# Half of a token tile's up side moved from matmuls to gathered rows

## The chip, the core and the metric

The kernel runs on one core of a Trainium2 chip. TensorE multiplies matrices (PE in the rows; PEld are its weight loads), VectorE (DVE) and ScalarE (ACT) work on elements, GpSimd (POOL) issues the gathers, SyncE (SP) issues most other transfers. The metric is the device time of one execution in microseconds; the kernel before takes 1613.15 us, the median of three runs (1612.51 to 1615.19).

## What is computed

One decoder layer on 512 tokens of width 1024, in float32: adaptive scale and shift, two kinds of attention, output projection, a norm, and then PEER, a layer of 16384 one-row experts. Each token has 8 heads, each head picks 16 experts, and the layer sums over these 128 picks:

```python
q = (hx @ w_pq).reshape(PEER_CHUNK, PEER_HEADS, 2, PEER_HALF)
sc = jnp.einsum('thpd,hpnd->thpn', q, sub_keys)
v_half, i_half = lax.top_k(sc, PEER_TOPK)
...
top_s, top_pos = lax.top_k(cand, PEER_TOPK)
idx = jnp.take_along_axis(cand_idx, top_pos, axis=-1)
g = jax.nn.softmax(top_s, axis=-1)
a = jax.nn.gelu(jnp.einsum('thkd,td->thk', u_tab[idx], hx))
return jnp.einsum('thk,thkd->td', (g * a), v_tab[idx])
```

`u_tab` is the up side (one dot product for a token and an expert), `v_tab` the down side (one row added for a token and an expert). A second norm ends the layer.

## The kernel before

The 512 tokens are four tiles of 128 (t = 0 to 3). Attention, the output projection and the first norm run first; `post_x` writes each tile's normed rows and, for tile 0, the expert layer's input `h2` by rows to memory. The product-key stage then multiplies by `w_pq`, and VectorE finds the best 16 of each half (`top16`). The first up blocks already stand beside it.

The expert stage treats tile 0 and tiles 1 to 3 in two ways.

Tiles 1 to 3 go densely over all 16384 experts, in 128 blocks of 128. An up block (`u_block`) loads 512 KB of `u_T`, splits it into a high and a low float32r part (`split`: ScalarE L80, VectorE L81), does 24 matmuls of 384 moving columns into the bank `st` (`mm3`, L90 to L92: three products for each of eight pieces of the width), and ScalarE's GELU writes the activations `a_r` (L756). A down block (`v_block`) loads and splits 512 KB of `v_blk`, multiplies the activations with the gate for each token and expert (`w`, L811), splits that too (L816, L817), and `v_mm` does 18 matmuls of 512 columns into six banks that add up over all blocks.

The dense gate comes from `topk` (the selection of one tile: indices `i01` and weights `g`) and `make_g`: for eight tokens at a time VectorE makes one-hot matrices (L671, L673), ScalarE scales one of them with eight instructions (L677), TensorE multiplies them, and ScalarE and VectorE copy the result to `stage` (L684), which goes to `g_d` in memory. Each such eight tokens is a gate unit; a tile has 16. `g_load` reads the gates back for eight blocks at a time.

Tile 0 takes its experts by gather (`gather_tile`): for each of the 128 picks, GpSimd's indirect transfer (L722) brings one row of `u_tab` to each of the 128 tokens, VectorE makes the dot product (L728), and later rows of `v_tab` are added with their weights (L738), in a ring of four buffers.

Three loops set the order. The first runs NB + NS = 32 + 24 up blocks ahead; after each, generators give out some of the selections, of the gate units (GRATE = 1.25 a block) and of the gathers, by a budget in microseconds (`pull`). Activations of 32 blocks stay in a ring; those of NS blocks go to `a_d` in memory by SP's queue (`keep`). The second part runs 72 pairs of an up and a down block with a gather budget of 3.2 us a pair, and the last 56 down blocks run alone with 1.2 us each. All engines take their instructions in a fixed order; `paced` ties the gathers' arithmetic to the blocks.

Of the kernel before, what the change touches and what calls it, by code (L numbers as in the profile page):

```python
# [20 lines left out]
P = 128  # L21
D = 1024
S = 512
# [15 lines left out]
NS = 24  # L39
GRATE = 1.25  # L40
LAST = 6


@with_exitstack
def layer(ctx: ExitStack, tc: tile.TileContext, A, out, dbg=None):
# [18 lines left out]
    h2_d = dram.tile([P, D], F32, name="h2_d")  # L64
    g2_d = dram.tile([1, D], F32, name="g2_d")
    a_d = [dram.tile([P, TD], F32, name=f"a_d{e}") for e in range(NS)]
# [431 lines left out]
    def post_x(t, pre, x1):  # L498
        nc.vector.tensor_mul(x1, pre, ln1g)
        nc.vector.tensor_add(x1, x1, ln1b)  # L500
        dma(x1_d[t], x1)
        if "x1" in dbg:
            dma(dbg["x1"][t * P:(t + 1) * P, :], x1)
        if t == 0:
            sc2row = row_of(lt, scale2, "rowtmp")
            h2 = pre
            nc.vector.tensor_mul(h2, x1, sc2row)
            sh2row = row_of(lt, cols(3), "rowtmp")
            nc.vector.tensor_add(h2, h2, sh2row)
            dma(h2_d, h2)  # L510
            g2row = row_of(lt, cols(5), "rowtmp")
            dma(g2_d, g2row[0:1, :])

    ln = {}
# [20 lines left out]
    sel = ctx.enter_context(tc.tile_pool(name="sel", bufs=1, reuse_waits="tile"))  # L535
# [50 lines left out]
    psB = ctx.enter_context(tc.tile_pool(name="psB", bufs=1, space=bass.MemoryType.PSUM, reuse_waits="tile"))  # L586
    ring_stack = ExitStack()
    ring = ring_stack.enter_context(tc.tile_pool(name="ring", bufs=1, side="right", reuse_waits="tile"))
    gath = ctx.enter_context(tc.tile_pool(name="gath", bufs=1, reuse_waits="tile"))
# [3 lines left out]
    def accbank():  # L593
        return psB.tile([P, 512], F32, name="acc", tag="acc", bufs=6)

    def topk(t, pool):
# [32 lines left out]
        i01 = sel.tile([P, 2, H, K16], F32, name="i01", tag="i01", bufs=2)  # L629
# [13 lines left out]
        g = sel.tile([P, H, K16], F32, name="g", tag="g", bufs=2)  # L643
# [49 lines left out]

    def all_topk(pool):
        for t in (1, 0, 2, 3):
            best[t] = yield from topk(t, pool)

    def all_g(pool, tk):
        for t in range(1, NT):
# [4 lines left out]
    acc0 = gath.tile([P, D], F32, name="acc0")  # L704
    h2n = gath.tile([P, D], F32, name="h2n")
    dma(h2n, h2_d)

    def gather_tile(pool):
        i01, g = best[0]
        ef = gath.tile([P, P], F32, name="ef")  # L710
        nc.vector.scalar_tensor_tensor(ef, i01[:, 0].rearrange("p h k -> p (h k)"), float(NKEY),
                                       i01[:, 1].rearrange("p h k -> p (h k)"), op0=OP.mult, op1=OP.add)
        ei = gath.tile([P, P], I32, name="ei")
        nc.vector.tensor_copy(ei, ef)
        w0 = gath.tile([P, P], F32, name="w0")
        nc.vector.tensor_copy(w0, g.rearrange("p h k -> p (h k)"))
        dots = gath.tile([P, P], F32, name="dots")
        yield 0.6

        def fetch(tab, j):  # L720
            b = gath.tile([P, D], F32, name="gb", tag="gb", bufs=4)
            nc.gpsimd.indirect_dma_start(out=b, out_offset=None, in_=A[tab],  # L722
                                         in_offset=bass.IndirectOffsetOnAxis(ap=ei[:, j:j + 1], axis=0))
            return b

        for j in range(P):
            b = fetch("u_tab", j)
            paced(nc.vector.scalar_tensor_tensor(b, b, 1.0, h2n, op0=OP.mult, op1=OP.mult,  # L728
                                                 accum_out=dots[:, j:j + 1]))
# [224 lines left out]
```

## Time and profile before

| what | value |
|---|---|
| median of three runs | 1613.15 us |
| the profiled execution, its span | 1615.1 us |
| TensorE, matmuls busy | 1536.0 us (95%) |
| VectorE busy | 1247.1 us (77%) |
| ScalarE busy | 760.0 us (47%) |
| GpSimd busy | 378.1 us (23%) |
| moved by DMA | 394.98 MB, mean 245 GB/s |

The shares are averages over stages with different work. Matmuls are pipelined and their ends are modelled, so the pace of TensorE is better read from their starts. A busy share of the DMA engines can come out a little over 1 in a short stretch.

### The profile page before, as it was taken

To read this page: it belongs to the slowest core of one execution; us is meant where nothing else is said; L and a number is where in the kernel's file an instruction comes from. 1 tells how busy PE (TensorE), PEld (TensorE's weight loads), DVE (VectorE), ACT (ScalarE), POOL (GpSimd) and SP (SyncE) were. 2 spreads that over 40 slices of the span, in tenths; PEclk is the share of its full clock that TensorE was granted. 3 is DMA by queue.
4 is the path that set the end of the run, shared out by engine and by line. 5 is a ranking of instruction groups with operands and counts; after the bars stand their busy time and mean duration, and the time that the engine had idled before them with its cause. 6 is when DMAs were issued, how large, how long until landed. Compare 5 with 4: busy or idle time off the path is not lost.

```text
span 1615.1 us, 22297 instructions
## 1 busy us (share of the span) xinstructions
PE 1536.0 (95%) x7837; PEld 1340.0 (83%) x7837; DVE 1247.1 (77%) x2519; ACT 760.0 (47%) x1346; POOL 378.1 (23%) x274
## 2 busy tenths in 40 slices
PE   7999898999998989998899999999999999999997
PEld 5677776889888888998788999988988898888875
DVE  7897666999898887766777777777868776787687
ACT  2565533234897998963233333333333333333341
POOL 0000000000011010104444443444535442434200
PEclk9999999999999999999999999999999999999999
DMA  8855542223366465689989889899889996889962
GB/s 302 289 187 181 170 156 82 89 79 116 107 219 213 155 232 190 219 282 359 313 304 329 291 311 319 297 321 312 320 289 324 322 306 246 286 300 310 374 204 76
DMA packets 154497, 394.98 MB, mean 245 GB/s; under 512 B 12305, under 2 KB 69009, under 8 KB 151186
## 3 DMA queue, kind: packets, MB, share of 16 engines
q1 hardware_dynamic: 117522, 259.33, 47.2%
q0 software_dynamic: 36864, 134.23, 23.0%
q8 instruction: 61, 1.00, 0.2%
q14 instruction: 50, 0.41, 0.1%
HBM read 358.91 MB, written 34.61 MB: 244 GB/s over the span
## 4 chain that ended last, share of the span: by engine, by line
PE 62%; issue 10%; DVE 10%; ACT 9%; DMA 7%; POOL 2%; SPq 0%; DVEq 0%; POOLq 0%; ACTq 0%
PE acc L91 9%; PE acc L90 9%; PE acc L92 9%; PE st L92 6%; PE st L91 6%; PE st L90 6%; ACT go L677 5%; PE bank L90 4%; PE bank L91 4%; PE bank L92 4%; DMA raw<-u_T 2%; DMA a_b<-a_d 2%; DVE lo L81 2%; ACT stage L684 1%; POOL gb L722 1%
## 5 line engine op out<-in xcount | busy, mean ns | idle before, releaser
L80 ACT CAST hi<-raw 128x1024 fp32r<-128x1024 f32 x286 | 300.3, 1051 | 359.8 <-PE st L91 191.3
L81 DVE TENSOR_TENSOR lo<-raw,hi 128x1024 fp32r<-128x1024 f32 x286 | 348.3, 1219 | 94.8 <-ACT hi L80 94.4
L90 PE MATMUL st<-h2h,hi 128*128 128x384 f32 x1024 | 352.4, 344 | 9.7 <-ACT a_r L756 5.8
L92 PE MATMUL st<-h2h,lo 128*128 128x384 f32 x1024 | 350.9, 343 | 5.6 <-DVE lo L81 5.5
L91 PE MATMUL st<-h2l,hi 128*128 128x384 f32 x1024 | 349.5, 341 | 0.0
L722 POOL DMA_INDIRECT gb<-u_tab,ei x128 | 173.2, 1353 | 623.2 <-DVE gb L728 354.6
L91 PE MATMUL acc<-lo,wh 128*128 128x512 f32 x768 | 304.3, 396 | 3.2 <-DVE lo L81 3.0
L90 PE MATMUL acc<-hi,wh 128*128 128x512 f32 x768 | 303.5, 395 | 0.4 <-ACT hi L803 0.4
L92 PE MATMUL acc<-hi,wl 128*128 128x512 f32 x768 | 303.8, 396 | 0.0
L722 POOL DMA_INDIRECT gb<-v_tab,ei x128 | 194.9, 1523 | 269.8 <-DVE acc L738 250.5
L90 PEld LDWEIGHTS st<-h2h,hi 128*128 128x128 f32 x1024 | 196.2, 192 | 15.2 <-ACT a_r L756 7.4
L816 ACT CAST wh<-w 128x384 fp32r<-128x384 f32 x128 | 65.6, 514 | 292.0 <-PE acc L91 273.6
L92 PEld LDWEIGHTS st<-h2h,lo 128*128 128x128 f32 x1024 | 196.0, 191 | 8.3 <-DVE lo L81 8.3
L91 PEld LDWEIGHTS st<-h2l,hi 128*128 128x128 f32 x1024 | 196.0, 191 | 3.2
L91 PEld LDWEIGHTS acc<-lo,wh 128*128 128x128 f32 x768 | 144.3, 188 | 36.5 <-DVE lo L81 4.3
L92 PEld LDWEIGHTS acc<-hi,wl 128*128 128x128 f32 x768 | 144.3, 188 | 34.5
L817 DVE TENSOR_TENSOR wl<-w,wh 128x384 fp32r<-128x384 f32 x128 | 71.1, 556 | 131.5 <-ACT wh L816 131.5
L90 PEld LDWEIGHTS acc<-hi,wh 128*128 128x128 f32 x768 | 144.1, 188 | 32.4 <-ACT hi L803 0.8
L677 ACT ACTIVATE go<-oh,iT 128x128 f32<-128x128 bf16 x384 | 166.4, 530 | 5.9 <-DVE eq L637 3.2
L738 DVE SCALAR_TENSOR_TENSOR acc<-gb,w,acc 128x1024 f32<-128x1024 f32 x127 | 162.2, 1277 | 1.2 <-DMA gb<-v_tab,ei 1.1
L728 DVE SCALAR_TENSOR_TENSOR gb<-gb,h2n 128x1024 f32<-128x1024 f32 x128 | 154.1, 1217 | 7.6 <-DMA gb<-u_tab,ei 7.5
L681 PE MATMUL acc<-go,oh 128*128 128x128 f32 x768 | 123.1, 294 | 15.2 <-ACT go L677 10.2
(206 smaller groups left out, 1854.5 us busy)
## 6 DMA issues: line engine op xcount, KB each, us to landing
raw<-u_T SPq DMA_DIRECT2D x128, 512.0 KB, 5.2
raw<-v_blk SPq DMA_DIRECT2D x128, 512.0 KB, 4.5
wada<-w_adaT SPq DMA_DIRECT2D x48, 512.0 KB, 4.5
g_d<-stage SPq DMA_DIRECT2D x24, 1024.0 KB, 5.4
gl<-g_d SPq DMA_DIRECT2D x16, 1536.0 KB, 13.1
raw<-w_pqT SPq DMA_DIRECT2D x16, 512.0 KB, 3.5
raw<-w_inT SPq DMA_DIRECT2D x10, 512.0 KB, 4.3
a_d<-a_r SPq DMA_DIRECT2D x24, 192.0 KB, 4.1
```

The costliest lines, as they stand in the source:

```text
L80: nc.scalar.copy(hi, src)
L81: split.last = nc.vector.tensor_sub(lo, src, hi.bitcast(F32))
L90: nc.tensor.matmul(ps, lh, rh, start=first, stop=False)
L91: nc.tensor.matmul(ps, lh, rl, start=False, stop=False)
L92: nc.tensor.matmul(ps, ll, rh, start=False, stop=last)
L677: nc.scalar.activation(go[:, i, :], oh0[:, :, i], AF.Copy, scale=iT[:, 2, t0 + i:t0 + i + 1])
L681: nc.tensor.matmul(ps[:, i * P:(i + 1) * P], oh1[:, 4 * u + i, :], go[:, 4 * u + i, :], start=True, stop=True)
L722: nc.gpsimd.indirect_dma_start(out=b, out_offset=None, in_=A[tab], in_offset=bass.IndirectOffsetOnAxis(ap=ei[:, j:j + 1], axis=0))
L728: paced(nc.vector.scalar_tensor_tensor(b, b, 1.0, h2n, op0=OP.mult, op1=OP.mult, accum_out=dots[:, j:j + 1]))
L738: paced(nc.vector.scalar_tensor_tensor(acc0, b, w0[:, j:j + 1], acc0, op0=OP.mult, op1=OP.add))
L816: nc.scalar.copy(wh, w)
L817: pace[0], pace_next[0] = pace_next[0], nc.vector.tensor_sub(wl, w, wh.bitcast(F32))
```

## The change

The first 64 tokens of tile 1 leave the up matmuls, which now take the last 320 tokens (`T0U` = 192 to 512). Their 128 picks are dot products with gathered rows instead: since 64 tokens fill half of the partitions, each gather brings two experts of a token at once (picks 0 to 63 to partitions 0 to 63, picks 64 to 127 to the others), so that 64 gathers do (`gather_part`). The GELU of the dots, multiplied into tile 1's gate weights, enters `make_g(1)`: the dense gate of these tokens is then already weighted, and `v_block` copies it (on ScalarE) where the other columns are multiplied. The down side is dense for them as before.

So that this can be, tile 1 is selected first and its gate is built last; the order of selections is 1, 2, 3, 0. 32 + 56 = 88 up blocks run ahead (before 56), the gate units are spread at 0.8 a block, and the activations of the 56 go out from a ring of three buffers of their own, by ScalarE's queue. Gate loads go by ScalarE's queue too, one group ahead. The gather ring has five buffers. Budgets: 2.2 us a block for the new gathers, then 1.3 us; 3.6 us a pair; 1.9 us for a down block alone. While blocks run ahead, the banks are four for `st` and four for the rest; then two and six as before.

```diff
-NS = 24
-GRATE = 1.25
+NS = 56
+GRATE = 0.8
+HU = 64
+T0U = P + HU
+TU = S - T0U
+GBUF = 5
+RA = 2.2
+RB = 1.3
...
-        for t in (1, 0, 2, 3):
+        for t in (1, 2, 3, 0):
             best[t] = yield from topk(t, pool)
+            if t < 2:
+                lists[t] = numbers(t)
...
+    def gather_part():
+        ei = lists[1]
+        eip = gath.tile([P, HU], I32, name="eip")
+        nc.vector.tensor_copy(eip[0:HU], ei[0:HU, 0:HU])
+        dma(eip[HU:P], ei[0:HU, HU:P])
+        for r in range(2):
+            dma(h2n[r * HU:(r + 1) * HU], h2_d[1][0:HU])
+        dots = gath.tile([P, HU], F32, name="dots1")
+        for j in range(HU):
+            dot(fetch("u_tab", eip, j), dots[:, j:j + 1])
+            yield 1.25
+        nc.scalar.activation(dots, dots, AF.Gelu)
+        far = gath.tile([P, HU], F32, name="far")
+        dma(far[0:HU], dots[HU:P])
+        g = best[1][1].rearrange("p h k -> p (h k)")
+        nc.vector.tensor_mul(g[0:HU, 0:HU], g[0:HU, 0:HU], dots[0:HU])
+        nc.vector.tensor_mul(g[0:HU, HU:P], g[0:HU, HU:P], far[0:HU])
+        weighted.append(True)
+        yield 0.3
...
-        ps = psB.tile([P, TD], F32, name="st", tag="st", bufs=2)
+        ps = psq[0].tile([P, TU], F32, name="st", tag="st", bufs=psq[1])
         for k in range(KB):
-            mm3(ps, hi[:, k, :], lo[:, k, :], h2h[:, k, P:], h2l[:, k, P:], k == 0, k == KB - 1)
+            mm3(ps, hi[:, k, :], lo[:, k, :], h2h[:, k, T0U:], h2l[:, k, T0U:], k == 0, k == KB - 1)
...
+        if NB <= e < NB + NS:
+            a = ring.tile([P, TU], F32, name="a_s", tag="a_s", bufs=3)
+        else:
+            a = ring.tile([P, TU], F32, name="a_r", tag="a_r", bufs=NB)
...
-            dma(a_d[e - NB], acts[e])
+            nc.scalar.dma_start(a_d[e - NB], acts[e])
...
-        budget[0] = pull(tk, budget[0] + (1.8 if 1 not in best else 1.8))
-        if 1 in best:
+        budget[0] = pull(tk, budget[0] + (2.6 if 1 not in best else 1.6))
+        if 2 in best:
...
-        if 0 in best:
-            if gt is None:
-                gt = gather_tile(gp)
-            c2 = pull(gt, c2 + 0.8)
+        if 1 in lists:
+            c2 = pull(gt, c2 + (RA if not weighted else RB))
...
-        dma(gl, g_d.rearrange("g p i t -> p g (i t)")[:, :, e * TG:(e + GB) * TG])
+        nc.scalar.dma_start(gl, g_d.rearrange("g p i t -> p g (i t)")[:, :, e * TG:(e + GB) * TG])
...
-        nc.vector.tensor_mul(w.rearrange("p (g t) -> p g t", t=TG), a.rearrange("p (g t) -> p g t", t=TG),
-                             gl[:, :, i * TG:(i + 1) * TG])
+        nc.scalar.copy(w[:, 0:HU].rearrange("p (g t) -> p g t", t=TG), gl[:, 0:HU // TG, i * TG:(i + 1) * TG])
+        nc.vector.tensor_mul(w[:, HU:].rearrange("p (g t) -> p g t", t=TG), a.rearrange("p (g t) -> p g t", t=TG),
+                             gl[:, HU // TG:, i * TG:(i + 1) * TG])
...
-            c2 = pull(gt, c2 + 3.2)
+            c2 = pull(gt, c2 + 3.6)
         else:
-            c2 = pull(gt, c2 + 1.2)
+            c2 = pull(gt, c2 + 1.9)
```

`numbers`, `fetch` and `dot` are cut out of `gather_tile`. `post_x` also writes the input rows of the first 64 tokens of tile 1.

## Rows read from the trace of the kernel before

**Rows 1.** Windows: stretch, length, busy PE PEld DVE ACT POOL (instructions), PEclk, DMA share, GB/s.
```profile
364.00:413.00 49.00, 46.34 (x254) 45.99 (x253) 47.78 (x242) 23.86 (x28) 0.00 (x0) 0.93 0.36 117
413.00:716.00 303.00, 280.66 (x1713) 260.19 (x1713) 245.38 (x438) 273.81 (x530) 28.00 (x26) 0.98 0.58 200
716.00:756.00 40.00, 34.77 (x184) 33.81 (x183) 23.27 (x34) 12.19 (x20) 10.70 (x9) 0.91 1.02 358
756.00:1364.00 608.00, 601.67 (x2992) 540.92 (x2991) 456.21 (x572) 208.29 (x287) 270.75 (x187) 0.99 0.88 308
1364.00:1604.00 240.00, 237.98 (x1018) 190.56 (x1017) 185.28 (x239) 80.01 (x107) 60.36 (x38) 1.00 0.78 268
```

**Rows 2.** Timeline of TensorE: start us, length us, engine, line, operation, tile.
```profile
1000.11 0.39 PE L90 MATMUL acc<-hi,wh 128*128 128x512 f32 x1
...
1004.31 0.33 PE L90 MATMUL st<-h2h,hi 128*128 128x384 f32 x1
...
1008.49 0.39 PE L90 MATMUL acc<-hi,wh 128*128 128x512 f32 x1
```

**Rows 3.** Groups by line, 413 to 716: busy us, mean ns, idle before.
```profile
L677 ACT ACTIVATE go<-oh,iT 128x128 f32<-128x128 bf16 x384 | 166.4, 530 | 5.9 <-DVE eq L637 3.2 <-DVE oh L671 2.1 <-PE acc L681 0.6
...
L673 DVE TENSOR_TENSOR oh<-iT,iota 128x1024 f32<-128x1024 f32 x48 | 58.2, 1212 | 1.1 <-ACT iT L663 1.1
L684 ACT COPY stage<-acc 128x512 f32<-128x512 f32 x48 | 50.6, 1054 | 0.0
...
L81 DVE TENSOR_TENSOR lo<-raw,hi 128x1024 fp32r<-128x1024 f32 x39 | 47.3, 1220 | 9.8 <-ACT hi L80 9.8
L80 ACT CAST hi<-raw 128x1024 fp32r<-128x1024 f32 x40 | 42.3, 1063 | 9.0 <-PE st L91 4.4 <-issue 2.8 <-DVE eq L634 1.2
L671 DVE TENSOR_TENSOR oh<-iTb,iota 128x1024 bf16<-128x1024 bf16 x48 | 32.9, 688 | 33.3 <-ACT go L677 33.3
...
L728 DVE SCALAR_TENSOR_TENSOR gb<-gb,h2n 128x1024 f32<-128x1024 f32 x22 | 26.7, 1217 | 0.0
L756 ACT ACTIVATE a_r<-st 128x384 f32<-128x384 f32 x39 | 19.5, 499 | 6.8 <-DMA a_d<-a_r 6.7
```

**Rows 4.** Timeline of TensorE in the gate stretch.
```profile
702.18 1.95 PE L681 MATMUL acc<-go,oh 128*128 128x128 f32 x16
...
703.88 0.42 PE L90 MATMUL st<-h2h,hi 128*128 128x384 f32 x1
```

**Rows 5.** Timeline of VectorE among the last down blocks.
```profile
1438.99 1.28 DVE L738 SCALAR_TENSOR_TENSOR acc<-gb,w,acc 128x1024 f32<-128x1024 f32 x1
1440.18 1.22 DVE L81 TENSOR_TENSOR lo<-raw,hi 128x1024 fp32r<-128x1024 f32 x1
1441.32 0.55 DVE L811 TENSOR_TENSOR w<-a_r,gl 128x384 f32<-128x384 f32 x1
```

**Rows 6.** Timeline of SP's queue: an activation sent out.
```profile
625.98 0.32 SPq L761 DMA_DIRECT2D a_d<-a_r  x1
```

**Rows 7.** Transfers: a queue's packets, MB, share; issues with KB each, us to landing.
```profile
q0 software_dynamic: 36864, 134.23, 23.0%
...
raw<-u_T SPq DMA_DIRECT2D x128, 512.0 KB, 5.2
...
gl<-g_d SPq DMA_DIRECT2D x16, 1536.0 KB, 13.1
...
a_b<-a_d SPq DMA_DIRECT2D x24, 192.0 KB, 4.3
```

**Rows 8.** Windows of two 20 us stretches of heavy transfers, columns as in rows 1.
```profile
780.00:800.00 20.00, 16.95 (x84) 14.97 (x84) 10.29 (x16) 4.43 (x7) 5.87 (x5) 0.99 0.98 342
1500.00:1520.00 20.00, 20.00 (x87) 16.09 (x87) 15.03 (x18) 6.89 (x10) 6.71 (x4) 1.00 1.03 405
```

**Rows 9.** Waits: who for whom, us in total, times, longest us.
```profile
DVE oh L671 <- ACT go L677: 33.3, 28, 2.9
...
ACT a_r L756 <- DMA a_d<-a_r: 20.2, 6, 7.9
```

More of the change, by code (lines that the diff above doesn't have):

```diff
@@ L63, in layer @@
     x1_d = [dram.tile([P, D], F32, name=f"x1_d{t}") for t in range(NT)]
-    h2_d = dram.tile([P, D], F32, name="h2_d")
+    h2_d = [dram.tile([P, D], F32, name=f"h2_d{t}") for t in range(2)]
     g2_d = dram.tile([1, D], F32, name="g2_d")
-    a_d = [dram.tile([P, TD], F32, name=f"a_d{e}") for e in range(NS)]
+    a_d = [dram.tile([P, TU], F32, name=f"a_d{e}") for e in range(NS)]
     g_d = dram.tile([NTG, P, NKEY, TG], F32, name="g_d")
@@ L692, in layer, with numbers @@
     budget = [0.0]
+    acc0 = gath.tile([P, D], F32, name="acc0")
+    h2n = gath.tile([P, D], F32, name="h2n")
+    w0 = gath.tile([P, P], F32, name="w0")
+    weighted = []
+    def numbers(t):
+        i01, g = best[t]
+        ef = gath.tile([P, P], F32, name="ef", tag="ef", bufs=1)
+        nc.vector.scalar_tensor_tensor(ef, i01[:, 0].rearrange("p h k -> p (h k)"), float(NKEY),
+                                       i01[:, 1].rearrange("p h k -> p (h k)"), op0=OP.mult, op1=OP.add)
+        ei = gath.tile([P, P], I32, name=f"ei{t}")
+        nc.vector.tensor_copy(ei, ef)
+        return ei
     def all_topk(pool):
-        for t in (1, 0, 2, 3):
+        for t in (1, 2, 3, 0):
             best[t] = yield from topk(t, pool)
+            if t < 2:
+                lists[t] = numbers(t)
+                if t == 0:
+                    nc.vector.tensor_copy(w0, best[0][1].rearrange("p h k -> p (h k)"))
+                yield 0.5
     def all_g(pool, tk):
-        for t in range(1, NT):
+        for t in (2, 3):
             while t not in best:
@@ L702, in all_g @@
             yield from make_g(t, pool)
[L704 to L724, printed above, removed]
+        while not weighted:
+            yield
@@ new lines, in all_g, with fetch, dot @@
+        yield from make_g(1, pool)
+    lists = {}
+    def fetch(tab, idx, j):
+        b = gath.tile([P, D], F32, name="gb", tag="gb", bufs=GBUF)
+        nc.gpsimd.indirect_dma_start(out=b, out_offset=None, in_=A[tab],
+                                     in_offset=bass.IndirectOffsetOnAxis(ap=idx[:, j:j + 1], axis=0))
+        return b
+    def dot(b, acc):
+        paced(nc.vector.scalar_tensor_tensor(b, b, 1.0, h2n, op0=OP.mult, op1=OP.mult, accum_out=acc))
+    def gather_part():
[17 more added lines that the diff above has]
+        yield 0.3
@@ L726, in gather_tile @@
+    def gather_tile():
+        ei = lists[0]
+        dots = gath.tile([P, P], F32, name="dots0")
+        dma(h2n, h2_d[0])
         for j in range(P):
-            b = fetch("u_tab", j)
-            paced(nc.vector.scalar_tensor_tensor(b, b, 1.0, h2n, op0=OP.mult, op1=OP.mult,
-                                                 accum_out=dots[:, j:j + 1]))
+            dot(fetch("u_tab", ei, j), dots[:, j:j + 1])
             yield 1.25
@@ L739, in gather_tile, with gathers @@
             yield 1.2
+    def gathers():
+        yield from gather_part()
+        while 0 not in lists:
+            yield None
+        yield from gather_tile()
     def pull(gen, us):
@@ L743, in pull @@
             try:
-                us -= next(gen)
+                cost = next(gen)
             except StopIteration:
                 return us
+            if cost is None:
+                return 0.0
+            us -= cost
         return us
@@ L768, in layer @@
     c1 = c2 = 0.0
-    gt = None
+    gt = gathers()
     for e in range(NB + NS):
@@ L778, in layer @@
                 drain(gg, 1)
-        if 0 in best:
-            if gt is None:
-                gt = gather_tile(gp)
-            c2 = pull(gt, c2 + 0.8)
+        if 1 in lists:
+            c2 = pull(gt, c2 + (RA if not weighted else RB))
+    pull(tk, 1e9)
+    while not weighted:
+        next(gt)
     drain(gg)
     g_stack.close()
+    sel_stack.close()
+    psB_stack.close()
+    psq[:] = ctx.enter_context(tc.tile_pool(name="psC", bufs=1, space=bass.MemoryType.PSUM, reuse_waits="tile")), 2, 6
     v_stack = ExitStack()
```

41 lines of the change are left out of this document (23 added, 18 removed).

## The prediction

> **What bounds the kernel now.** I read the busy time of the engines by stretch first, then the starts of single matmuls, then the groups of the costly stretch, then the transfers. The stretches [rows 1] cut the span where the work changes. From 364 to 413 the product-key stage ends on VectorE (47.78 of 49 us busy) while the first up blocks already run. From 413 to 716 the gates of tiles 1 to 3 are built beside up blocks: ScalarE is busy 273.81 of 303 us. Then eight plain up blocks follow until 756. From 756 to 1364 run 72 pairs of an up and a down block with TensorE busy 601.67 of 608 us, and to 1604 the last 56 down blocks with TensorE full again. The tail is 11 us.
>
> So TensorE bounds the last 850 us, and ScalarE with VectorE the gate stretch. For TensorE the reader should look at starts, not at the busy time, which overlaps: 18 down matmuls of 512 columns start between 1000.11 and 1004.31, 24 up matmuls of 384 columns from there to 1008.49 [rows 2]. That is 0.233 us and 0.174 us for one, 4.20 us for a down block, 4.18 us for an up block, 8.38 us for a pair. 72 pairs would be 603 us; the stretch took 608.
>
> In the gate stretch I add up means [rows 3]. One gate unit (eight tokens; 48 of them) costs ScalarE 166.4/48 = 3.47 us of scaling plus one stage copy, 4.52 us. With the 42.3 us of high parts, 19.5 us of GELU and some 20 us of selection copies and table loads ScalarE has 299 us of work in 303 us. TensorE has only 38 up blocks (159 us) and the 768 gate passes there. Sixteen passes with sixteen weight loads took 1.70 us, 702.18 to 703.88 [rows 4], so all of them are 82 us. TensorE's own work is 241 of 303 us: 60 us of slack that only more up work could fill.
>
> **The change, part by part.**
>
> *Narrower up matmuls.* The moving side falls from 384 to 320 columns in all 3072 up matmuls. Spacing goes with the columns in the two rows that show it: 0.454 ns a column at 384, 0.456 at 512 [rows 2]. At 320 that is 0.145 us. Bounds: 0.174 (nothing gained) and 0.144 (by the slope between the two). The weight load is no floor there, since the gate passes carry a 128x128 load each at 0.106 us [rows 4]. I take 0.145: an up block becomes 3.48 us, a pair 7.68, and the 128 blocks save 90 us of TensorE time.
> The Trainium skill, "TensorE: Matmul & The Clock Gate", section "Back-to-back issue gap", speaks against this: it gives sustained spacings of about 81 ns at 128 columns and 131 ns at 512. By that slope, 0.13 ns a column, 64 columns would save 8 ns a matmul, 26 us in all instead of 90. This trace disagrees with it: 233 ns at 512 and 174 ns at 384 [rows 2].
>
> *32 more up blocks ahead, 88 instead of 56.* These move into the stretch with TensorE slack. But they bring work for the others, and so do the 64 new gathers with a dot product each. I followed the generators' own costs through the loop to place them. Tile 1's selection ends at block 6 (before: 9), all selections at block 38, the 64 dots at block 42, the 48 gate units at block 78 (0.8 a block against 1.25 before). 48 of tile 0's 128 dots fall ahead of the first down block (before: 24).
>
> Durations on VectorE, by starts: 1.14 us for a low part, 1.19 us for a weighted row added [rows 5]; a dot is a 1.22 us instruction with a read of the accumulator, 1.15 us by the same overlap. A gate unit is 1.21 + 0.69 us of means and a stage copy like ScalarE's of 1.05 [rows 3], 2.73 by starts. What is left of 245.38 us busy [rows 1] after 39 low parts, 48 units and 22 dots [rows 3] is 45 us for some two and a half selections, 18 us each.
> - To 413 us: VectorE sets the pace and still has the same product-key work, so I keep 413, now with 7 blocks done.
> - Blocks 7 to 38, on VectorE: 31 low parts 35 us, 55 dots 63 us, three selections 54 us, 17 units 46 us, together 198 us. At the busy share of the stretch that VectorE does bound, 0.975 [rows 1], 203 us. TensorE has 31 x 3.48 + 17 x 1.7 = 137 us there, ScalarE some 145. Ends at 616.
> - Blocks 38 to 78, on ScalarE: 31 units x 4.52 = 140 us, 40 x (1.05 high part + 0.44 GELU by 320 columns) = 60 us, and 40 sends of activations. These are moved from SP's queue to ScalarE's. The trace shows no issue on ScalarE; on SP one takes 0.32 us [rows 6], and here it also waits for its GELU. Bounds 0 and 0.8 us; I take 0.32, 13 us. Sum 213 us, at the 0.99 of the stretch before 215 us. TensorE: 40 x 3.48 + 31 x 1.7 = 192 us; VectorE some 180 us (40 low parts, 31 units, 45 dots). Ends at 831.
> - Blocks 78 to 88: TensorE 3.5 us each, 35 us. Ends at 866.
> Bounds of this stage: 849 if every bounding engine runs without a gap, 907 if VectorE in blocks 7 to 38 gets only the 0.81 of the gate stretch before [rows 1].
>
> *40 pairs.* TensorE 40 x 7.68 = 307 us. VectorE: two low parts, the two products (0.55 us at 384 columns [rows 5], some 0.95 together) and 2.9 gathered rows, 6.6 us of 7.7. Transfers: up and down block 0.524 MB each, an eighth of the gate load 0.197 MB [rows 7], and 117 gathers in 40 pairs by the loop's budget of 3.6 us (before 3.2), of 134.23/256 = 0.524 MB each, 1.53 MB a pair: 2.78 MB. In 7.68 us that is 362 GB/s, and the pairs before moved 308 at a busy share of 0.88 [rows 1]. What can the engines give? Full stretches gave 358 (716 to 756 [rows 1]) and 342 (780 to 800 [rows 8]); 1500 to 1520 gave 405, with the large loads of the end. The mix is nearest to the first two; I take 355. Then a pair takes 7.83 us, 313 us in all: to 1179.
>
> *88 down blocks alone.* 4.20 us each on TensorE. Gathers run at 1.9/1.2 = 1.58 a block (before 1.0) until they end at block 97; from block 72 a stored activation of 0.164 MB is read too (56 instead of 24; before 0.192 MB [rows 7]). Blocks 40 to 72 move 1.55 MB, at 355 GB/s 4.37 us; blocks 72 to 97 1.72 MB, 4.83 us; the last 31 take 4.20. Sum 140 + 121 + 130 = 391 us, 21 over TensorE's 370: to 1570. VectorE has 4.0 us a block there, under the 4.4 to 4.8.
>
> *Small things.* The copy of the 64 weighted columns goes to ScalarE, about 0.25 us a block, and the product on VectorE shrinks by 0.08; ScalarE is busy a third there [rows 1]. The gate loads move from SP's queue to ScalarE's, one group ahead; behind such a load, where its buffer is still in use, the next high part on ScalarE waits, at most one down product each. The activations sent out get three buffers of their own. Before, GELU waited 20.2 us for such sends [rows 9]; most of that lay where ScalarE had slack, so I count no gain, up to 10 us. The reload of the token rows between the two families of dots, and the moved half of the GELU results, can each stop VectorE for a landing of some 4 us: bounds 0 and 9, I take 5 together with the start of the down blocks, where the stretch before lost 5 us against 603. VectorE's 33.3 us of waiting for scaled rows [rows 9] should shrink, since units come more thinly; nothing counted. Two more row products for the second tile in the norm stage are under 2.5 us and are offset by the three fewer low parts before 413.
>
> **Sum.** 413 + 203 + 215 + 35 + 313 + 391 + 5 + 11 = 1586 us of span. The profiled run's span of 1615.1 is 2 us above the median of 1613.15, so 1584; I write 1585. Of the 90 us of shorter matmuls and the slack filled ahead, most is spent on the work taken in.
>
> **The rivals.**
> - *Transfers decide, slower side.* In the pairs and in blocks 40 to 97 some 204 MB must pass. SP's raw loads, ScalarE's loads and the gathers share 16 engines, and a late gather holds the low parts behind it on VectorE. Price: at 342 GB/s 325 + 400 us, 1606; at 330 337 + 410 us, 1628. It is slower than before below about 338 GB/s. For it: 342 in a full stretch, and TensorE at 16.95 of 20 us there [rows 8]. Against it: 358 over 40 us [rows 1]. Chance 0.19.
> - *Transfers don't bind.* The new mix gets what 1500 to 1520 got: 307 + 370 us, 1558. For it: TensorE was full in that stretch [rows 8]. Against: those were large rows, and the long stretches come to some 350 GB/s at full share (308/0.88 [rows 1]). Chance 0.20.
> - *VectorE's order binds ahead.* In blocks 7 to 38 dots, selections, units and low parts stand in one queue, and one wait holds them all; at 0.81 busy this part takes 244 us, 1626. It decides below 0.86. For it: the 33.3 us wait [rows 9]. Against: that wait came from a full ScalarE. Chance 0.12.
> - *The narrower matmul isn't shorter*, the change not doing what it says: then blocks 78 to 88 keep 4.18, pairs 8.38 us, and blocks 38 to 78 are TensorE's at 220 us and some gaps: 7 + 22 + 16 us more, 1630. If it had a third of the saving (the page's rule above) about 1615. Against: both rows go with the columns. Chance 0.03.
>
> **How the numbers follow.** The forecast, 1565 to 1608, has 0.46. Faster by over 0.2% (about what can be told from no change) means under 1610: forecast 0.45, unbound transfers 0.20, and the mild parts of the others 0.02: 0.67. Within 0.2%: 0.08. Slower: 0.25. The range leaves out the best end (ahead stage at 849 and unbound transfers, 1541) and the worst of two bad cases together (1670): 1548 to 1640.
>
> **What would show it.** Right: up matmuls start 0.145 us apart; the first down matmul after block 88 near 866 us, with VectorE 95% busy from 413 to 616; pairs near 7.8 us at a transfer share of 1.0 and 350 GB/s or more; down blocks of 4.4 to 4.8 us until the gathers end, then 4.2. Wrong: down blocks starting past 900 us, a spacing over 0.15 us, or pairs over 8.1 us with raw loads or gathers as releasers.

## The result and the profile after

The changed kernel takes 1598.44 us (median of four runs, 1588.19 to 1601.17); the kernel before, run beside it, takes 1614.02. The ratio is 0.9886, with a 95% interval of 0.9854 to 0.9918: about 1.1% faster. The forecast was 1585 us, or 1.8%. The profiled execution has a span of 1599.4 us, and the readings below are made against that.

First the head of the page of the changed kernel (busy us, share of the span, instructions), then its stretches, cut where its own work changes. The columns of the second fence are those of [rows 1].

```profile
span 1599.4 us, 22711 instructions
...
PE 1459.3 (91%) x7837; PEld 1272.5 (80%) x7837; DVE 1309.6 (82%) x2654; ACT 782.3 (49%) x1475; POOL 486.7 (30%) x338
```

```profile
413.00:616.00 203.00, 158.92 (x907) 144.39 (x907) 184.54 (x414) 121.88 (x213) 77.99 (x56) 0.89 0.75 261
616.00:842.00 226.00, 215.48 (x1549) 210.58 (x1547) 193.32 (x248) 194.73 (x378) 87.76 (x50) 1.00 0.93 336
842.00:950.00 108.00, 94.72 (x532) 87.43 (x533) 90.04 (x136) 41.35 (x69) 59.07 (x42) 0.92 0.99 360
950.00:1190.00 240.00, 240.00 (x1320) 216.88 (x1319) 204.69 (x259) 96.02 (x160) 127.05 (x88) 1.00 0.98 357
1190.00:1463.00 273.00, 252.22 (x1050) 203.57 (x1050) 224.46 (x270) 97.68 (x173) 119.37 (x81) 0.94 0.96 341
1463.00:1588.00 125.00, 122.34 (x534) 99.68 (x533) 79.28 (x115) 44.89 (x81) 1.09 (x2) 1.00 0.58 181
```

Before, TensorE was all but full in the last 850 us, and its idle time lay in the gate stretch and the eight blocks behind it [rows 1]. Now it stands idle mostly in three places: 44 us in 413 to 616, where VectorE is busy 184.54 of 203 us; 13 us in 842 to 950, around the first down block; and 21 us in 1190 to 1463, in the first two thirds of the down blocks alone. The DMA share went from 0.88 in the pairs [rows 1] to 0.96 to 0.99 from 842 to 1463. Work was taken off TensorE; VectorE is busy 0.91 of the first of these places, and the transfers 0.96 to 0.99 of the other two.

The length of single matmuls is read from starts again. This is TensorE's timeline of the changed kernel in the pairs (start us, length us, operation):

```profile
1040.70 0.39 PE L96 MATMUL acc<-hi,wh 128*128 128x512 f32 x1
...
1044.81 0.30 PE L96 MATMUL st<-h2h,hi 128*128 128x320 f32 x1
...
1048.32 0.39 PE L96 MATMUL acc<-hi,wh 128*128 128x512 f32 x1
```

24 up matmuls take 3.51 us, 0.146 us each against 0.174 before [rows 2], and 18 down matmuls 4.11 us. A pair is 7.62 us.

At the seam between the stages ahead and the pairs VectorE has a wait of 15.69 us. First the timelines there, of SP, ScalarE, TensorE and VectorE (idle time before the instruction and its releaser in brackets; ACTq and SPq are the issues on the queues of ScalarE and SP), then a row of who waited for whom over the whole span (us in total, times, longest), which is used further down:

```profile
825.55 0.33 SPq L699 DMA_DIRECT2D g_d<-stage  x1
835.64 0.42 ACTq L853 DMA_DIRECT2D gl<-g_d  x1
836.16 0.77 ACT L812 ACTIVATE a_s<-st 128x320 f32<-128x320 f32 x2 [7.31 <-DMA g_d<-stage]
836.63 7.13 ACTq L817 DMA_DIRECT2D a_d<-a_s  x2
843.85 1.04 ACT L86 CAST hi<-raw 128x1024 fp32r<-128x1024 f32 x1 [6.92 <-issue]
844.95 0.64 PE L96 MATMUL st<-h2h,hi 128*128 128x320 f32 x1 [6.81 <-ACT hi L86]
846.61 0.49 DVE L875 TENSOR_TENSOR w<-a_r,gl 128x320 f32<-128x320 f32 x1 [15.69 <-DMA gl<-g_d]
```

```profile
ACT hi L86 <- DMA raw<-v_blk: 71.8, 24, 8.7
```

VectorE stood 15.69 us for the first gate load, with the low parts behind it. That load is issued when the last gate's store has landed, 10 us after the store's own issue. On ScalarE a GELU stood 7.31 us behind the load's issue. Then the issue of the next two activations on the same queue took 7.13 us, where a send later on this queue takes 0.33; the next high part stood 6.92 us behind them, and TensorE 6.81 us for that high part. The first down matmul starts at 878.4 us, 12 us later than the forecast of 866.

### The profile page after: what moved, and what is told of

Same layout as the page of the kernel before. It is cut to its first block, busy times and chain, and to the rows that moved or that the text cites. A ratio compares the mean times of both kernels' runs of the same rounds, so it can differ in the third digit from the quotient of the medians.

```text
span 1599.4 us, 22711 instructions
## 1 busy us (share of the span) xinstructions
PE 1459.3 (91%) x7837; PEld 1272.5 (80%) x7837; DVE 1309.6 (82%) x2654; ACT 782.3 (49%) x1475; POOL 486.7 (30%) x338
## 4 chain that ended last, share of the span: by engine, by line
PE 49%; DMA 14%; issue 14%; DVE 13%; POOL 4%; ACT 4%; SPq 0%; POOLq 0%; DVEq 0%; ACTq 0%
DMA gl<-g_d 7%; PE acc L97 7%; PE acc L98 7%; PE acc L96 7%; PE bank L96 4%; PE bank L97 4%; PE bank L98 4%; POOL gb L741 4%; PE st L98 3%; PE st L96 3%; PE st L97 3%; DVE lo L87 2%; PE acc L692 2%; DMA gb<-u_tab,ei 2%; DVE gb L746 2%
## 5 line engine op out<-in xcount | busy, mean ns | idle before, releaser
L86 ACT CAST hi<-raw 128x1024 fp32r<-128x1024 f32 x286 | 299.2, 1050 | 278.5 <-DMA raw<-v_blk 71.8
L96 PE MATMUL st<-h2h,hi 128*128 128x320 f32 x1024 | 330.5, 323 | 33.0 <-ACT hi L86 33.0
L98 PE MATMUL st<-h2h,lo 128*128 128x320 f32 x1024 | 328.3, 321 | 23.0 <-DVE lo L87 22.8
L97 PE MATMUL st<-h2l,hi 128*128 128x320 f32 x1024 | 325.3, 318 | 0.0
L96 PE MATMUL acc<-hi,wh 128*128 128x512 f32 x768 | 304.3, 396 | 11.3 <-ACT hi L86 11.1
L741 POOL DMA_INDIRECT gb<-u_tab,ei x128 | 204.1, 1595 | 229.0 <-DVE gb L746 213.0
L746 DVE SCALAR_TENSOR_TENSOR gb<-gb,h2n 128x1024 f32<-128x1024 f32 x192 | 231.0, 1217 | 17.3 <-DMA gb<-u_tab,ei 9.6
L741 POOL DMA_INDIRECT gb<-v_tab,ei x128 | 183.9, 1437 | 193.2 <-DVE acc L782 176.3
L96 PEld LDWEIGHTS st<-h2h,hi 128*128 128x128 f32 x1024 | 200.5, 196 | 39.0 <-ACT hi L86 37.3
L97 PEld LDWEIGHTS st<-h2l,hi 128*128 128x128 f32 x1024 | 200.1, 195 | 1.5
L688 ACT ACTIVATE go<-oh,iT 128x128 f32<-128x128 bf16 x384 | 169.0, 524 | 33.9 <-DVE oh L682 26.9
L741 POOL DMA_INDIRECT gb<-u_tab,eip x64 | 88.8, 1387 | 280.3 <-DVE cand L555 148.7
L104 POOL TENSOR_TENSOR rs_r<-rs_v,mhalf 128x1 f32<-128x1 f32 (+1 forms) x12 | 9.3, 775 | 399.8 <-DVE rs_v L102 364.2
```

The lines of the kernel that those rows point to most:

```text
L86: nc.scalar.copy(hi, src)
L96: nc.tensor.matmul(ps, lh, rh, start=first, stop=False)
L97: nc.tensor.matmul(ps, lh, rl, start=False, stop=False)
L98: nc.tensor.matmul(ps, ll, rh, start=False, stop=last)
L104: nc.gpsimd.tensor_tensor(r, v, mhalf.to_broadcast([P, n]), op=OP.pow)
L688: nc.scalar.activation(go[:, i, :], oh0[:, :, i], AF.Copy, scale=iT[:, 2, t0 + i:t0 + i + 1])
```

## The experiments

Each run asks what one part of the change is worth. Medians are given with the range of the runs; ratios are to the kernel before, run on the same chip, with a 95% interval. The experiments ran on four chips, on which the kernel before had medians of 1611.65 to 1617.74 us. So two versions are best compared by their ratios, times 1614 us, and a difference of a few us between them decides nothing.

**The price of the new dots.** Of the 64 gathers with a dot product, one is left; the kernel leaves out the other 63.

```diff
-        for j in range(HU):
+        nc.vector.memset(dots, 0.0)
+        for j in range(1):
             dot(fetch("u_tab", eip, j), dots[:, j:j + 1])
             yield 1.25
+        for j in range(HU - 1):
+            yield 1.25
```

> The changed kernel with one of the 64 new gathers and dots instead of all (the gate weights of half of tile 1 are then wrong, everything else is computed). Theory 1 (VectorE sets the pace in blocks 7 to 38): 55 dots x 1.15 = 63 us less for VectorE there, of which some 45 are gained until ScalarE or TensorE sets the pace: block 38 near 575 instead of 623, end 1550 us. Rival (TensorE and ScalarE wait on each other there, not on VectorE): block 38 gains under 20 us, end above 1580 us.

Measured: 1537.94 us (1532.72 to 1542.66), ratio 0.9512 [0.9475, 0.9549]. That is 60 us under the changed kernel. All of it is gained by block 38, in the stretch in which VectorE sets the pace: the GELU of that block stands at 561 us instead of 623, and that of block 78 at 776 instead of 836. In the window from 413 to 616 of this kernel TensorE is busy 190.72 us instead of 158.92:

```profile
413.00:616.00 203.00, 190.72 (x1294) 184.68 (x1295) 169.27 (x349) 172.69 (x319) 14.98 (x13) 0.97 0.59 203
```

But this run takes away VectorE's work and 33 MB of transfers at once. The next one keeps the gathers and cuts the dots to 64 of their 1024 columns.

```diff
-            dot(fetch("u_tab", eip, j), dots[:, j:j + 1])
+            b = fetch("u_tab", eip, j)
+            paced(nc.vector.scalar_tensor_tensor(b[:, 0:64], b[:, 0:64], 1.0, h2n[:, 0:64], op0=OP.mult, op1=OP.mult,
+                                                 accum_out=dots[:, j:j + 1]))
```

> The changed kernel with all 64 new gathers but dots over 64 columns instead of 1024 (so the gates of half of tile 1 are wrong): VectorE's 63 us ahead go, the 33.5 MB of transfers stay. If VectorE's time is the price of the gathers: within 12 us of the run without them, 1538 to 1550 us. If the transfers or the gathers' latency are: 1580 to 1598 us.

Measured: 1549.12 us (1544.61 to 1553.7), ratio 0.9589 [0.9556, 0.9622]. By the ratios that is 48 us under the changed kernel. So some 48 of the 60 us are VectorE's time in the dots. The other 12 stay with the gathers and with what is left of the dots, which are short but not gone; these two were not separated. The groups from 413 to 616, first of the changed kernel, then of this one (busy us, mean ns, idle before), show the time taken off:

```profile
L746 DVE SCALAR_TENSOR_TENSOR gb<-gb,h2n 128x1024 f32<-128x1024 f32 x56 | 67.5, 1216 | 2.9 <-DMA gb<-u_tab,eip 2.9
```

```profile
L758 DVE SCALAR_TENSOR_TENSOR gb<-gb,h2n 128x64 f32<-128x64 f32 x62 | 13.0, 221 | 11.1 <-DMA gb<-u_tab,eip 11.1
```

A dot falls from 1216 to 221 ns. For 64 of them that is 64 us of instruction time, and some 48 us reach the end. The short dots still take 13.0 us, and the waits for gathers rise from 2.9 to 11.1 us, since VectorE now gets there sooner.

**The worth of the narrower matmuls.** The changed kernel with the up side at its old width of 384 columns; the 64 extra columns are computed and not read.

```diff
-        ps = psq[0].tile([P, TU], F32, name="st", tag="st", bufs=psq[1])
+        ps = psq[0].tile([P, TD], F32, name="st", tag="st", bufs=psq[1])
...
-            mm3(..., h2h[:, k, T0U:], h2l[:, k, T0U:], ...)
+            mm3(..., h2h[:, k, P:], h2l[:, k, P:], ...)
...
-        nc.scalar.activation(a, ps, AF.Gelu)
+        nc.scalar.activation(a, ps[:, HU:], AF.Gelu)
```

> The changed kernel with up matmuls of 384 columns again; the first 64 columns of each result are not used. Nothing else differs. Theory 1 (the narrower matmul pays in full only where TensorE sets the pace: the ten blocks before the seam and the pairs; ahead of that VectorE and ScalarE set it): +0.70 us on 40 pairs and 10 blocks and some 15 us in blocks 38 to 78, 1640 to 1650 us. Rival A (the pairs are transfer-bound, the width is worth little): under 1620 us. Rival B (TensorE sets the pace everywhere): 128 x 0.70 = 90 us, 1688 us.

Measured: 1640.64 us (1639.58 to 1642.11), ratio 1.0144 [1.0117, 1.0170]: 42 us more than the changed kernel. The narrower matmul saves some 86 us of TensorE's time (3072 times 0.028 us, by the starts above) and 42 us of the span. Where they arrive can be read from the starts in the two traces: the kernel with 384 columns is 3 us behind at the GELU of block 38, 19 at that of block 78, 21 at the first down matmul and 44 at the last up matmul. Up to block 38, where VectorE sets the pace, the saving is lost almost whole; in the pairs most of it arrives.

**The other part: 88 blocks ahead without the gathers.** First the plain version, the kernel before with larger numbers: 56 blocks sent out instead of 24, gate units spread to suit, the gather rates adapted.

```diff
-NS = 24
-GRATE = 1.25
+NS = 56
+GRATE = 0.8
...
-            c2 = pull(gt, c2 + 0.8)
+            c2 = pull(gt, c2 + 1.3)
...
-            c2 = pull(gt, c2 + 1.2)
+            c2 = pull(gt, c2 + 1.3)
```

> The kernel before with 88 up blocks ahead instead of 56 and gate units at 0.8 a block instead of 1.25 (gather budgets 1.3 us where they were 0.8 and 1.2, so that the gathers still end in time); no other part of the change. Theory 2 (the slack of the gate stretch is what the change wins, the tile 1 gathers only cost): 60 us of TensorE slack filled, some 20 us lost again to sends that share the ring's one free place and SP's queue: 1575 to 1590 us. Rival (the ring and SP's queue stop GELU at each of 56 sends): 1610 us or more.

Measured: 1624.59 us (1619.28 to 1630.82), ratio 1.007 [1.0046, 1.0095]. Slower: 88 blocks ahead are no gain by themselves. Then the same with the rings and queues that the change brings, but no gathers for tile 1: NB 24 and NS 64, three buffers for activations on their way out, their sends and the gate loads on ScalarE's queue, gate loads one group ahead. The order of the selections, the banks, the four gather buffers and the gather budget of a pair stay those of the kernel before. Beside the edit above:

```diff
-        a = ring.tile([P, TD], F32, name="a_r", tag="a_r", bufs=NB + 1)
+        if NB <= e < NB + NS:
+            a = ring.tile([P, TD], F32, name="a_s", tag="a_s", bufs=3)
+        else:
+            a = ring.tile([P, TD], F32, name="a_r", tag="a_r", bufs=NB)
...
-            dma(a_d[e - NB], acts[e])
+            nc.scalar.dma_start(a_d[e - NB], acts[e])
...
-        dma(gl, g_d.rearrange("g p i t -> p g (i t)")[:, :, e * TG:(e + GB) * TG])
+        nc.scalar.dma_start(gl, g_d.rearrange("g p i t -> p g (i t)")[:, :, e * TG:(e + GB) * TG])
...
-        if order[n] % GB == 0:
-            gl = g_load(order[n])
+        if n % GB == 0 and n + GB < NKEY:
+            gls[order[n + GB]] = g_load(order[n + GB])
```

> As e5_ahead, with the sent activations in three buffers of their own and sent by ScalarE's queue (24 kept and 64 sent, for space), and the gate loads on ScalarE's queue, one group ahead: all of the change but the tile 1 gathers. By the two runs on the change (narrower matmuls worth 42 us, the 64 gathers and dots costing 60 us) it should be 18 us faster than the changed kernel: 1575 to 1585 us. Rival (without the narrower matmul TensorE is too full to gain): 1600 us or more.

Measured: 1596.65 us (1596.31 to 1602.65), ratio 0.9905 [0.9875, 0.9934]. That cannot be told from the whole change (0.9886 [0.9854, 0.9918]). So the part that names the change, half a tile by gather, comes out at about nothing: the dots and gathers take 60 us, and 42 us of narrow matmuls, with somewhat quicker down matmuls (last section), can give about as much back. That this is the whole balance is argued, since the two kernels also differ in the points just named. The gain over the kernel before is had without it. The run still missed its expected 1575 to 1585. Its windows show the same kind of loss as the whole change in the down blocks, though TensorE stands idle less there, 14 us in 1190 to 1463 instead of 21:

```profile
413.00:616.00 203.00, 190.13 (x1164) 182.28 (x1164) 183.95 (x354) 175.67 (x324) 39.30 (x32) 0.97 0.71 244
...
950.00:1190.00 240.00, 240.00 (x1206) 216.74 (x1205) 181.00 (x204) 83.89 (x117) 98.25 (x71) 1.00 0.88 308
1190.00:1463.00 273.00, 258.81 (x1089) 206.51 (x1087) 202.89 (x242) 87.47 (x119) 97.68 (x64) 0.97 0.92 320
```

From the end of the last pair (1192.1) to the last matmul (1583.8) 88 down blocks take 392 us; at its own pace TensorE would need 370. A last run on this version takes the gathers earlier, to empty the down blocks of them.

```diff
-            c2 = pull(gt, c2 + 1.3)
+            c2 = pull(gt, c2 + (0.8 if 3 not in best else 1.7))
...
-            c2 = pull(gt, c2 + 3.2)
+            c2 = pull(gt, c2 + 4.0)
...
-            c2 = pull(gt, c2 + 1.3)
+            c2 = pull(gt, c2 + 1.0)
```

> As e6_ahead_rings, with the gathers of tile 0 moved forward: ahead 0.8 us a block until the selections end, then 1.7; 4.0 us a pair; 1.0 us for a down block alone (was 1.3, 3.2, 1.3). In e6_ahead_rings down blocks 40 to 97 took 276 us where TensorE needs 239, at 314 to 325 GB/s. If the transfers ask too much there: those 37 us shrink to under 12, pairs stay at 8.4 us, end at 1565 to 1578 us. Rival (the small pieces of gate and activation loads cost, not the gathers; or the pairs now stall): 1590 us or more.

Measured: 1593.53 us (1593.35 to 1594.6), ratio 0.9879 [0.9859, 0.9899]. The down blocks alone do get shorter, 379 us instead of 392. But the last up matmul falls at 1197.7 instead of 1187.7: 3 us are paid ahead and 7 in the pairs. The whole cannot be told from the run before it. Gathers can be moved, and here their cost moved along.

**The queue of the gate loads.** The forecast counted nothing for the move of the gate loads from SP's queue to ScalarE's. Here it is undone in the changed kernel.

```diff
-        nc.scalar.dma_start(gl, g_d.rearrange("g p i t -> p g (i t)")[:, :, e * TG:(e + GB) * TG])
+        dma(gl, g_d.rearrange("g p i t -> p g (i t)")[:, :, e * TG:(e + GB) * TG])
```

> The changed kernel with the gate loads on SP's queue again, still one group ahead. Theory 1 (at the seam ScalarE stands behind its own issue of the first gate load, 7.3 us, and gate loads on a ring of their own land late among full transfers): 1575 to 1590 us, ScalarE's wait for g_d gone. Rival (the transfers are full, whichever queue holds the gate load; behind it raw loads are now late): 1595 to 1610 us, with raw loads as releasers in place of gate loads.

Measured: 1635.7 us (1634.18 to 1640.77), ratio 1.0122 [1.009, 1.0153]: 37 us slower than with the move, slower than the kernel before. The expected gain was wrong; its rival, raw loads late behind the gate loads, holds at more than its price. The windows of the pairs and of the down blocks, and one row of its waits:

```profile
950.00:1190.00 240.00, 230.97 (x1251) 207.14 (x1250) 191.86 (x248) 90.30 (x151) 121.48 (x83) 0.99 0.95 341
1190.00:1463.00 273.00, 239.53 (x998) 193.86 (x997) 210.63 (x244) 90.73 (x161) 137.58 (x86) 0.93 0.92 327
```

```profile
ACT hi L86 <- DMA raw<-v_blk: 114.5, 27, 13.6
```

TensorE is no longer full in the pairs, the rate falls from 357 to 341 GB/s, and the high parts wait 114.5 us for raw down blocks instead of 71.8, 13.6 us at worst. At the seam the run is 6 us sooner (first down matmul at 872.9); it loses 23 us in the pairs and 16 in the down blocks alone. A gate load is 1536 KB, three raw blocks [rows 7], and SP's timeline shows the raw load behind it held at its issue:

```profile
972.37 0.40 SPq L853 DMA_DIRECT2D gl<-g_d  x1
976.16 7.59 SPq L92 DMA_DIRECT2D raw<-v_blk  x1
983.84 0.38 SPq L92 DMA_DIRECT2D raw<-u_T  x1
```

Others take 0.33 us. From 950 to 1460 this run has such an issue behind every gate load, of 4.9 to 9.5 us; with the gate loads on ScalarE's queue the longest raw issue there is 0.56. SP also stood 16.8 us in ten waits for a free gate buffer; that part was not separated. The same move in the kernel before, where with the queue the date changes too, from where the gates are needed to one group ahead:

```diff
-        dma(gl, g_d.rearrange("g p i t -> p g (i t)")[:, :, e * TG:(e + GB) * TG])
+        nc.scalar.dma_start(gl, g_d.rearrange("g p i t -> p g (i t)")[:, :, e * TG:(e + GB) * TG])
...
-        if order[n] % GB == 0:
-            gl = g_load(order[n])
+        if n % GB == 0 and n + GB < NKEY:
+            gls[order[n + GB]] = g_load(order[n + GB])
```

> The kernel before with the gate loads on ScalarE's queue, one group ahead; nothing else. In the changed kernel going back to SP's queue cost 37 us. If that is because raw loads stood behind gate loads while the transfers are full: little here, where pairs moved 308 GB/s, 1605 to 1614 us. Rival (the queue itself is worth it at any load): 1575 to 1590 us.

Measured: 1612.86 us (1605.55 to 1620.08, ten runs), ratio 1.0007 [0.9988, 1.0026]: nothing. Yet the kernel before shows the same held issues in its pairs, of 4.9 to 7.7 us:

```profile
1051.20 0.38 SPq L793 DMA_DIRECT2D gl<-g_d  x1
1052.75 7.66 SPq L86 DMA_DIRECT2D raw<-u_T  x1
```

TensorE was busy 601.67 of 608 us there all the same [rows 1]. So with 308 GB/s and a share of 0.88 the raw loads had the room to catch up, and at 0.98 they had not. That it is the share that decides is argued from these two kernels, which differ in more than that.

**VectorE's order ahead.** From 413 to 616 the changed kernel has these groups on VectorE, and this wait (us in total, times, longest):

```profile
L695 DVE COPY stage<-acc 128x512 f32<-128x512 f32 x16 | 16.9, 1054 | 15.5 <-PE acc L692 15.5
```

```profile
DVE stage L695 <- PE acc L692: 15.5, 16, 2.3
```

One of the two stage copies of a gate unit is VectorE's. It works 16.9 us at them and stands 15.5 us for the gate passes of TensorE, with dots, selections and low parts behind it. ScalarE is busy only 121.88 of 203 us there. The edit gives tile 2's copies, the units of that stretch, to ScalarE.

```diff
-                    (nc.scalar.copy if u == 0 else nc.vector.tensor_copy)(
+                    (nc.scalar.copy if u == 0 or t == 2 else nc.vector.tensor_copy)(
```

> The changed kernel with both copies of a gate result on ScalarE while tile 2's units are made (before: one on VectorE, 16 units x 1.05 us), the stretch in which VectorE sets the pace and ScalarE is busy 122 of 203 us. If VectorE's time there is what counts: block 38 some 12 to 16 us sooner, end at 1582 to 1588 us. Rival (the waits between the engines count, not the work): within 5 us of 1598.

Measured: 1579.18 us (1570.66 to 1582.3), ratio 0.977 [0.9737, 0.9804], 19 us under the changed kernel and faster than both. Its ScalarE group from 413 to 616, the wait of VectorE there, and its window:

```profile
L695 ACT COPY stage<-acc 128x512 f32<-128x512 f32 x34 | 34.6, 1071 | 2.1 <-PE acc L692 1.8
```

```profile
DVE stage L695 <- PE acc L692: 0.7, 1, 0.7
```

```profile
413.00:616.00 203.00, 171.02 (x1011) 156.09 (x1012) 186.25 (x424) 150.72 (x261) 82.57 (x60) 0.91 0.82 286
```

The wait is gone, the GELU of block 38 comes at 604 us instead of 623, and the first down matmul at 859.9 instead of 878.4. What was gained at block 38 is kept to the end. Both the 16.9 us of copying and the 15.5 us of waiting left VectorE's queue; how the 19 us divide between them was not separated.

**The gather rate of the down blocks.** The changed kernel with its gathers spread more thinly behind the pairs, and the same together with the copies on ScalarE.

```diff
-            c2 = pull(gt, c2 + 1.9)
+            c2 = pull(gt, c2 + 1.45)
```

> The changed kernel with a gather budget of 1.45 us for a down block alone instead of 1.9, so that the gathers end near block 116 instead of 97. Theory 1 (blocks 40 to 97 ask for more than the transfers give, 1.55 to 1.72 MB in 4.2 us): the waits from block 57 to 90 shrink, 1575 to 1588 us. Rival (the late gate loads come from their small pieces, not from the gathers): within 4 us of 1598.

Measured: 1595.04 us (1586.15 to 1598.44), ratio 0.985 [0.9808, 0.9893]; 3.4 us less, and the intervals overlap. Not decided.

> e9_copies with the gather budget of e3_even (1.45 us for a down block alone instead of 1.9). The two act in different stretches, ahead and in down blocks 40 to 97, so they should add: 11 us sooner at down block 97, some of it lost where the gathers now go on, 1570 to 1577 us. Rival (what the down blocks win by this is lost in their last third, as the small gain of e3_even alone says): 1576 to 1582 us.

Measured: 1573.8 us (1572.23 to 1576.13), ratio 0.9746 [0.973, 0.9762]. This is the fastest version, 2.5% under the kernel before and 23 us, by the ratios, under the change as it came. Against the copies alone it is 5 us, again with intervals that touch: the two runs together make a small gain from the even rate likely, and no more.

**The seam.** If VectorE's 15.69 us are a gate load that comes too late because the gates are finished too late, gate units at 0.95 a block instead of 0.8 should take them away.

```diff
-GRATE = 0.8
+GRATE = 0.95
```

> The changed kernel with gate units at 0.95 a block instead of 0.8, so that the last gate is written some 10 blocks sooner before the first down block. Theory (the seam's 15.7 us of VectorE and 7.3 us of ScalarE wait for the first gate load): the first gate load is issued without a wait and both waits go, 1580 to 1588 us. Rival (what is saved at the seam is lost ahead, where the units stand closer on ScalarE, or the seam is the transfers'): 1595 to 1602 us.

Measured: 1608.65 us (1597.48 to 1617.29, ten runs), ratio 0.9962 [0.9936, 0.9988], slower than the change. VectorE's timeline at the seam:

```profile
821.82 0.49 DVE L875 TENSOR_TENSOR w<-a_r,gl 128x320 f32<-128x320 f32 x1 [16.54 <-DMA gl<-g_d]
```

The gates and the first gate load do come sooner, by some 24 us. So does the instruction that needs the load, and it waits 16.54 us as before. Meanwhile block 38 comes at 631 instead of 623 and block 78 at 851 instead of 836; VectorE has 18 gate units from 413 to 616 instead of 16. The theory fell. The wait goes with the order in which the seam is written, not with the gates' date. The two traces show its parts: the last gate's store is issued at 825.55 us in the changed kernel and at 802.01 here, the load 10.1 us later in both, and the product follows 11.0 and 9.7 us after that. VectorE's last copy of a gate ends just before the store, and little else stands between that and the product. What would shorten the wait was not tried.

## Why the prediction was right or wrong, step by step

The direction was right, and the time lies 13 us above the forecast and inside its range. The sum, by its terms:

- **Spacing of the narrow matmul: right.** 0.145 us forecast, 0.146 measured. Of the two prices, spacing that goes with the columns is the one that holds; the rival in which the matmul isn't shorter had 1630 us, and the kernel made that way, with 384 columns, took 1640.64.
- **To block 38: 616 forecast, 623 measured.** VectorE does bound this part, as forecast: 63 dots fewer brought block 38 forward by 62 us. The busy share of 0.975 was too high; it got 184.54/203 = 0.91. This is the rival "VectorE's order binds ahead" in a mild form: one wait in the queue, the stage copies', took 15.5 us. I had looked at the 33.3 us wait for scaled rows [rows 9] and priced the copies by their own time alone.
- **Block 38 to 78: 215 forecast, 213 measured** (623 to 836). Right.
- **Block 78 to the first down matmul: 35 forecast, 42 measured (836.2 to 878.4), and 5 us of "small things" that were far more.** The 42 hold the first pair's up block, 3.5 us, which the forecast counts with the pairs. The 5 us held the start of the down blocks. From 842 to 950 TensorE alone lost 13 us, and VectorE stood 15.69 us for one gate load. I had written that behind a gate load only a high part waits, for a down product at most; that the first product of the stage itself needs the load, with VectorE's low parts behind it, I did not follow through. Nor did I count the two sends behind that load, which held ScalarE and with it TensorE for some 7 us.
- **The pairs: 313 forecast, 311 measured** (878.4 to 1189.6). The total is right by luck, by two errors that cancel. I had the transfers bind at 355 GB/s and 7.83 us a pair. They ran at 357 and TensorE was full at 7.62 us from 950 on; the extra time lies in the first pairs, at the seam.
- **88 down blocks alone: 391 forecast, 396 measured** (1189.6 to 1586.1). The total is near, its parts are not. TensorE ran a down block in 4.08 us here, 359 us in all, so 37 us are lost instead of 21. These are the windows of blocks 40 to 72 and 72 to 97, and a wait in the second (us in total, times, longest):

```profile
1189.60:1321.00 131.40, 131.02 (x577) 107.94 (x576) 120.90 (x141) 52.13 (x93) 76.94 (x50) 1.00 0.99 360
1321.00:1457.40 136.40, 116.00 (x452) 91.32 (x452) 98.43 (x122) 44.33 (x77) 42.47 (x33) 0.89 0.95 331
```

```profile
DVE w L875 <- DMA a_b<-a_d: 30.1, 9, 8.1
```

  In blocks 40 to 72 I had the transfers bind, 140 us; TensorE was full, and they took 131. Nearly the whole loss lies in blocks 72 to 97, where the stored activations are read back: 121 us forecast, 136 measured, 5.45 us a block instead of 4.83. I had priced these 0.164 MB by the rate alone. VectorE's gate product waited 30.1 us for them to land, TensorE stood idle 20 us, and its mean granted clock there was 0.89. With the gathers spread more thinly (the run with 1.45 us a block) the gate products still wait 33.9 us for stored activations from block 72 to 97, so thinner gathers did not take this wait away; a run that loads the activations earlier was not made. The 331 GB/s of this stretch speak for the rival "transfers decide", the 360 before it against it.
- **The gate loads' queue: nothing counted, where 37 us hang on it.** My price of full transfers, 355 GB/s without a word on the raw loads that stand behind a gate load, was in effect that of the loads moved. For a kernel that kept them on SP's queue the same working would have given the same 1585, against a measured 1635.7.
- **The balance, "most is spent on the work taken in": right, and more than most.** Of the shorter matmuls 42 us come through, the dots and gathers cost 60, and 88 blocks ahead with their rings and queues alone give as much as the whole change.

Summed, against the forecast span of 1586: 12 us at the first down matmul, 2 less in the pairs, 6 more in the down blocks, 2 more in the tail (1586.1 to 1599.4), less the 5 us that stand in these instead of by themselves: 1599. Some luck is in this: down matmuls 3% quicker than in the kernel before (last section) were in no step, and what they gave hid a part of what the steps missed.

What stays open: which of the rings, the sends on ScalarE's queue and the gate loads there turns 1624.59 into 1596.65 in the version without gathers. They were moved together; the 37 us of the gate loads are shown for the changed kernel alone. What would close the seam is open too, and how much of the down blocks' 37 us the gather rate, or an earlier load of the stored activations, could give back.

## What to carry to other kernels

Shortening the bounding engine's work pays only in the stretches in which it still bounds afterwards: of some 86 us here 42 arrived, and the work that bought them cost 60. Count that work on the engine that will bind next, by its queue and each wait in it, and not by busy time alone: 17 us of copies were worth 19, with a wait of 15.5 us that went with them. When the DMA share comes near 1, look at what stands behind the largest load on each queue: the move was worth nothing in a kernel with a share of 0.88 in its pairs, and 37 us in one with 0.98. Price a small load that the next product needs by when it lands, not by its bytes.

## What the runs showed of the hardware that was not expected

- The pairs moved 357 GB/s over 240 us at a share of 0.98 with TensorE busy all the time, and down blocks 40 to 72 moved 360 at 0.99 with TensorE full; blocks 72 to 97, at 0.95, moved 331 while TensorE stood idle 20 us of 136. A share near 1 does not by itself say that TensorE starves.
- The issue of the transfer right behind a gate load on the same queue is slow. Behind every gate load in the pairs it took 4.9 to 7.7 us on SP's queue in the kernel before, and 4.9 to 9.5 us from 950 to 1460 with the gate loads back on SP; on ScalarE's queue the two sends behind the first gate load took 7.13 us, and ScalarE stood 6.92 us behind them. A usual issue takes 0.33. What in the gate load makes it so was not tried.
- A down matmul of 512 columns starts every 0.233 us in the kernel before [rows 2] and in the version without gathers, but every 0.227 us in most of the changed kernel. These are TensorE's timelines near the end, 36 matmuls each, first of the changed kernel, then of the version without gathers:

```profile
1519.72 0.39 PE L98 MATMUL acc<-hi,wl 128*128 128x512 f32 x1
...
1527.88 0.39 PE L98 MATMUL acc<-hi,wl 128*128 128x512 f32 x1
```

```profile
1519.73 0.40 PE L92 MATMUL acc<-hi,wl 128*128 128x512 f32 x1
...
1528.13 0.40 PE L92 MATMUL acc<-hi,wl 128*128 128x512 f32 x1
```

  8.16 us against 8.40. The trace splits cleanly: all versions made from the changed kernel have 0.227 (the one with wide up matmuls too, so it is not the width), all made from the kernel before have 0.233. The matmuls of the down product are written alike in both. Over 128 blocks of 18 it comes to 15 us of TensorE's time that no step of the forecast had. The cause is open, and how much of it reaches the end was not separated.
- TensorE's mean granted clock is 0.89 from 413 to 616, where it waits for VectorE, against 0.97 and more in the full stretches; with the dots taken out, and TensorE busy 190.72 us, it is 0.97 in the same stretch. A mean of 0.89 lies between its two levels (1.2 and 2.4 GHz). The forecast took the gate passes there at their price in a stretch of 0.98 [rows 1, 4]. VectorE waited for them in the stage copies, so the lower clock can be a part of those 15.5 us; that was not measured by itself.
